# One pass over the weights for both segments in w_out and the last w_down chunk, with every second scaled norm tile in PSUM

## Chip, cores and metric

The kernel runs on one core of a Trainium2 chip. The metric is device time in microseconds (us), the median of several runs. The profile is one further execution, recorded by the hardware profiler. Engines: PE is TensorE (PEld its weight loads), DVE is VectorE, ACT is ScalarE, POOL is GpSimd, SP issues the DMAs.

## What is computed

A two-layer diffusion trunk on 512 latent tokens and 256 context tokens of 1024 features. Each layer mixes tokens (attention of three kinds and a short convolution), projects the result with w_out, adds it to x with a gate, norms x, and runs a gated FFN with a convolution over the tokens. The parts that matter here, cut from the reference:

```python
def rmsnorm(x, w):
    return x * lax.rsqrt(jnp.mean(x * x, axis=-1, keepdims=True) + EPS) * w
...
for l in range(DEPTH):
    need_ctx = l < DEPTH - 1
    hl = modulate(rmsnorm(xl, norm_mix_w[l]), sh1, sc1) @ w_in[l]
    ...
    yl = jnp.concatenate([oa_l, ob_l, oc_l, od_l], axis=-1) @ w_out[l]
    xl = xl + g1 * yl
    fl = modulate(rmsnorm(xl, norm_ffn_w[l]), sh2, sc2)
    xl = xl + g2 * conv_ffn(fl, ffn_w_up[l], ffn_conv_w[l], ffn_conv_b[l], ffn_w_down[l])
    if need_ctx:
        ...
return rmsnorm(xl, final_norm_w)
```

In the cut, `oa_l` to `od_l` are the mixing's outputs, and the branch on `need_ctx` does the same for the context tokens. The context tokens pass through layer 0 and are only read in layer 1's mixing, so layer 1's w_out and FFN run over the 512 latent tokens alone.

## The kernel before

x lies feature-major: eight tiles `x[k]` of 128 features x 768 tokens. An fp32 product is made of three faster matmuls: a weight tile is split into a high part `wh` (a cast on ACT, L481) and the rest `wl` (a subtraction, L486, on POOL, or in the "fast" form 640 columns on DVE and 384 on POOL), an activation into `yh` and `yl` likewise, and `product` adds wh·yh, wh·yl and wl·yh for each of 8 blocks k of the contraction (24 matmuls a feature and segment; 21 in the last w_down chunk, which has 7 blocks). The weights come in the order of `unit_order`, through three `raw` buffers and two of each part.

Layer 0 works on the segments 0:512 and 512:768 (SEGS), layer 1 on 0:256 and 256:512 (HALVES). In four stages the program before makes two sweeps over the eight output features, one for each segment, and loads and splits the weights in each: w_out of layer 0, the last w_down chunk of layer 0, w_out of layer 1, and the last w_down chunk of layer 1. A product lands in a PSUM bank with the tag `tp` (there are two), and `residual` (L917, DVE) adds it to x.

After the first sweep, the norm of the first segment starts. `rstd_steps` squares x on ACT (L344), adds the eight squares on POOL and DVE (L353, the form that is not `direct`), sums over partitions with four small matmuls into `ms`, takes the root (L357, ACT) and the reciprocal (L358, DVE) and broadcasts it with four matmuls into a PSUM bank `rb` with the tag `pj` (there is one). `norm_apply` then makes for each feature tile the scaled tile `yt` = x·A·rb on DVE (L404), its high part on ACT (L408) and its low part on DVE (L414, even k) or POOL (L410 and L412, odd k). These steps are a generator; `tick` runs some of them behind each product of the second sweep and pins the DVE instructions in program order. The second segment is normed in the `direct` form (each square goes to PE, 8 groups of four `ms` matmuls), and `woven` puts its steps between pieces of the next products on the first segment: the first two FFN units (`up_open`, `up_product`), or the first w_in units. In layer 1's last stage the norm is the final one (`final`, L425), whose result `ot` goes out by DMA. `u` is a pool of six SBUF buffers that squares, `yt`, `ot` and FFN tiles share. In layer 0's FFN, rows of the modulation (`junk` and `mrow`, L311) are computed on DVE between units, in the pool `mrow`; they need `cbc`, which is loaded and put through a silu on ACT (L216) before the FFN.

Of the kernel before, what the change touches and what calls it, by code (L numbers as in the profile page):

```python
# [16 lines left out]
KT = 8  # L17
# [27 lines left out]
AHEAD_SCORES = 2  # L45
SCORE_SHARE = 0.4
# [6 lines left out]
class Trunk:  # L53
# [34 lines left out]
    def build(self):  # L88
# [53 lines left out]
        for j in range(4):  # L142
# [11 lines left out]
            for sg, rb in zip(SEGS, r):  # L154
                self.norm_apply(x, y, sg, self.amix[0], self.mod[0][:, 0:8], rb, ks)
# [14 lines left out]
        for l in range(DEPTH):  # L170
# [22 lines left out]
            y = None  # L193
# [12 lines left out]
            self.pin = ALL  # L206
            for u in first:
                part(u, 0, 8)()
# [10 lines left out]
            def after(sg, l=l, need=need, x=x, y2=y2):  # L219
                if need:  # L220
                    if not y2:
                        self.scale_vec(l + 1, self.amix[l + 1], O_NM, 8)
                        y2.extend(self.new_y())
                    steps = self.norm_steps(x, y2, sg, self.amix[l + 1], self.mod[l + 1][:, 0:8], sg != segs[0])
                    if sg == segs[0]:
                        self.pace = steps
                        self.tick(1)
                    else:
                        early = self.early_start(l + 1, True)
                        part = lambda n, k0, k1: lambda: self.early_products([early[n]], y2, SEGS[0], range(k0, k1))  # L230
                        self.woven(steps, part(0, 0, 4), part(0, 4, 8), part(1, 0, 8))
                        self.early_products(early[1:], y2, SEGS[1], range(KT))
                        self.split_weights(spare=True)
                    if sg[1] <= SEQ:
                        for k in range(KT):
                            nc.sync.dma_start(out=xd[:, k, sg[0]:sg[1]], in_=x[k][:, sg[0]:sg[1]])
                else:
                    self.pace = self.final(x, sg, sg != segs[0])
                    self.tick(1 if sg == segs[0] else 99)

            self.ffn(l, x, y, segs, first, todo, after)
# [124 lines left out]
    def norm_steps(self, x, y, sg, A, sh, direct=False):  # L366
        r = yield from self.rstd_steps(x, *sg, direct)
        for k in range(KT):
            self.norm_apply(x, y, sg, A, sh, r, [k])
            yield  # L370

# [24 lines left out]
    def norm_apply(self, x, y, sg, A, sh, r, ks):  # L396
        nc = self.nc
        a, b = sg
        n = b - a
        j = 0 if b <= SEQ else 1  # L400
        for k in ks:
            t = self.u.tile([128, T], F32, tag="u", name="yt")
            yh, yl, _ = y[k]
            i = nc.vector.scalar_tensor_tensor(out=t[:, :n], in0=x[k][:, a:b], scalar=A[:, k, j:j + 1],  # L404
                                               in1=r[:, :n], op0=ALU.mult, op1=ALU.mult)
            if self.ticking:
                self.tc.keep_in_program_order(i)
            nc.scalar.activation(out=yh[:, a:b], in_=t[:, :n], func=AF.Identity, bias=sh[:, k, j:j + 1])  # L408
            if self.slow and k % 2:
                nc.gpsimd.tensor_tensor(out=t[:, :n], in0=t[:, :n],  # L410
                                        in1=sh[:, k, j:j + 1].broadcast_to([128, n]), op=ALU.add)
                nc.gpsimd.tensor_tensor(out=yl[:, a:b], in0=t[:, :n], in1=f32v(yh[:, a:b]), op=ALU.subtract)  # L412
            else:
                nc.vector.scalar_tensor_tensor(out=yl[:, a:b], in0=t[:, :n], scalar=sh[:, k, j:j + 1],  # L414
                                               in1=f32v(yh[:, a:b]), op0=ALU.add, op1=ALU.subtract)

    def final(self, x, sg, direct):
# [3 lines left out]
        r = yield from self.rstd_steps(x, a, b, direct)  # L421
# [11 lines left out]
    def unit_order(self):  # L433

        for l in range(DEPTH):
            for u in UNITS:
                yield ("win", l, u)
            segs = SEGS if l < DEPTH - 1 else HALVES
            for _ in segs:
                for m in range(KT):  # L440
                    yield ("wout", l, m)
            for k0, k1 in CHUNKS:
                for i in range(k0, k1):
                    if i == 0:
                        yield ("wup", l, 0, 0)
                    yield ("wup", l, i, 1)
                    if i + 1 < NF:
                        yield ("wup", l, i + 1, 0)
                for _ in range(len(segs) if k1 == NF else 1):
                    for m in range(KT):  # L450
                        yield ("wdn", l, m, k0, k1)
# [469 lines left out]
    def w_out(self, l, s, x, sg):  # L921
        a, b = sg
        for m in range(KT):
            w = self.weights(("wout", l, m), b - a == 256, m % 3 == 2 and l == 0)
            p = self.bank("tp", "po")
            self.product(p[:, :b - a], w, s, a, b)
            self.residual(p, x, self.mod[l][:, 16:24], m, a, b)
            self.tick(2 if m < 3 else 1)
        self.tick(KT)
# [31 lines left out]
    def ffn(self, l, x, y, segs, first, todo, after):  # L961
# [10 lines left out]
        for k0, k1 in CHUNKS:  # L972
# [18 lines left out]
            sweeps = [[sg] for sg in segs] if k1 == NF else [cseg]  # L991
            for sweep in sweeps:
                for m in range(KT):
                    w = self.weights(("wdn", l, m, k0, k1), sweep[0][1] - sweep[0][0] == 256,
                                     k1 == NF and m % 3 == 2 and l == 1)
                    for a, b in sweep:
                        p = self.bank("tp", "pd")
                        if k1 < NF and a == SEQ:
                            self.product2(p, w, G, a, b)
                            self.residual(p, x, gate, m, a, b, 2)  # L1000
                        else:
                            self.product(p[:, :b - a], w, G, a, b)
                            self.residual(p, x, gate, m, a, b)
                    if todo and m % 2:
                        todo.pop(0)()
                    self.tick(2 if m < 3 else 1)
                self.tick(KT)
                if k1 == NF:
                    after(sweep[0])
# [439 lines left out]
```

## Time and profile before

| | |
|---|---|
| time, median of 3 runs | 1758.03 us (1757.46 to 1758.92) |
| time of the profiled execution | 1758.37 us, span 1756.6 us |
| PE busy | 1672.1 us, 95% |
| DVE, ACT, POOL busy | 952.0, 801.0, 1002.0 us |
| DMA | 244.15 MB, 139 GB/s |

PE is busy nearly all the time, so time is lost where PE waits, where its list has more matmuls than needed, or where its clock is granted at half speed. The chain of work that ended last runs through PE for the most part. The windows view shows the four stages one by one; the waits view says what PE waited for in them.

### The profile page before, as it was taken

What the parts mean: (1) busy time and instruction counts of PE and PEld (TensorE: products, weight loads), DVE (VectorE), ACT (ScalarE), POOL (GpSimd) and SP (SyncE); (2) the same over time, 40 slices, a digit from 0 to 9 for tenths busy, and PEclk for the clock granted to TensorE, in tenths of its full rate; (3) what the DMA queues carried; (4) which work ended last, traced back from release to release, by engine and by line L of the source; (5) the groups of instructions that cost most, each with busy time, mean ns of one, the idle gap of its engine ahead of it and who ended that gap; (6) DMA issues with size and microseconds to landing.
All of it is one profiled execution on the core that took longest, in us unless ns stands there. A gap on an engine that the chain in (4) does not pass through costs nothing. (4 is left out here: it accounts for less than half of the span.)

```text
span 1756.6 us, 26615 instructions
## 1 busy us (share of the span) xinstructions
PE 1672.1 (95%) x9740; PEld 1421.0 (81%) x9740; DVE 952.0 (54%) x1849; ACT 801.0 (46%) x1399; POOL 1002.0 (57%) x1348
## 2 busy tenths in 40 slices
PE   6899999899999999999999988999999999999997
PEld 4578878798878888888888877888879888888887
DVE  3577767562667754654355475877656422122245
ACT  4276766553443321332143354776654543242343
POOL 1424234776566654664467664434865776676763
PEclk9999999999999999999999999999999999999999
DMA  8566535336434433443333636453446323233334
GB/s 335 177 197 210 157 108 186 94 121 233 149 104 129 123 109 98 133 127 111 110 131 116 196 120 189 138 148 105 141 128 210 109 96 94 99 94 99 96 108 132
DMA packets 78450, 244.15 MB, mean 139 GB/s; under 512 B 9072, under 2 KB 12656, under 8 KB 78192
## 3 DMA queue, kind: packets, MB, share of 16 engines
q1 hardware_dynamic: 78320, 242.46, 43.6%
q8 instruction: 77, 1.26, 0.3%
q14 instruction: 53, 0.43, 0.1%
HBM read 214.64 MB, written 27.79 MB: 138 GB/s over the span
## 5 line engine op out<-in xcount | busy, mean ns | idle before, releaser
L486 POOL TENSOR_TENSOR wl<-raw,wh 128x256 fp32r<-128x256 f32 (+1 forms) x750 | 579.9, 803 | 556.1 <-ACT wh L481 528.5
L73 PE MATMUL pu<-y,wh 128*128 128x512 f32 (+1 forms) x1792 | 559.2, 388 | 4.2 <-DVE up L957 2.6
L481 ACT CAST wh<-raw 128x1024 fp32r<-128x1024 f32 (+1 forms) x228 | 233.6, 1027 | 353.8 <-PE pd L73 188.7
L73 PEld LDWEIGHTS pu<-y,wh 128*128 128x128 f32 x1792 | 331.8, 188 | 71.2 <-ACT wh L481 2.4
L73 PE MATMUL pu<-y,wl 128*128 128x512 f32 (+1 forms) x1072 | 369.0, 351 | 0.0
L73 PE MATMUL pj<-y,wh 128*128 128x512 f32 (+1 forms) x1216 | 325.4, 356 | 8.9 <-ACT ev L581 5.3
L73 PE MATMUL pd<-g,wh 128*128 128x512 f32 (+1 forms) x1048 | 290.2, 362 | 4.4 <-DVE x L917 2.8
L73 PEld LDWEIGHTS pj<-y,wh 128*128 128x128 f32 x1216 | 206.9, 192 | 39.1 <-ACT ev L581 8.2
L73 PEld LDWEIGHTS pu<-y,wl 128*128 128x128 f32 x1072 | 201.9, 188 | 31.1
L73 PEld LDWEIGHTS pd<-g,wh 128*128 128x128 f32 x1048 | 188.5, 193 | 34.2 <-ACT wh L481 4.0
L73 PE MATMUL pj<-y,wl 128*128 128x512 f32 (+1 forms) x608 | 212.0, 349 | 0.0
L954 DVE SCALAR_TENSOR_TENSOR up<-pu,par,up 128x511 f32<-128x511 f32 (+1 forms) x132 | 83.1, 658 | 231.4 <-ACT up L952 212.9
L73 PE MATMUL pd<-g,wl 128*128 128x512 f32 (+1 forms) x584 | 196.2, 342 | 2.9 <-DVE wl L486 2.8
L917 DVE SCALAR_TENSOR_TENSOR x<-pd,mod,x 128x256 f32<-128x256 f32 (+1 forms) x96 | 56.6, 592 | 168.9 <-PE pd L73 168.3
L73 PEld LDWEIGHTS pj<-y,wl 128*128 128x128 f32 x608 | 116.7, 192 | 14.5
L677 POOL TENSOR_TENSOR p<-p,rec 128x512 f32<-128x512 f32 (+2 forms) x80 | 79.5, 998 | 83.2 <-DVE rec L673 59.5
L73 PEld LDWEIGHTS pd<-g,wl 128*128 128x128 f32 x584 | 112.6, 193 | 17.3 <-DVE wl L486 3.5
L311 DVE SCALAR_TENSOR_TENSOR junk<-mrow,cbc 128x1024 f32<-128x1024 f32 x80 | 121.9, 1524 | 2.1 <-DMA mrow<-in_wmodt 1.3
L73 PE MATMUL po<-og,wh 128*128 128x256 f32 (+1 forms) x512 | 111.6, 314 | 3.9 <-ACT sq L344 2.5
L979 POOL TENSOR_TENSOR up<-up 128x256 f32<-128x256 f32 x105 | 105.3, 1028 | 1.4 <-DVE up L957 0.7
L748 DVE TENSOR_TENSOR wtl<-wtp,wth 128x512 fp32r<-128x512 f32 x132 | 87.4, 668 | 29.5 <-ACT wth L747 28.7
L73 PEld LDWEIGHTS po<-og,wh 128*128 128x128 f32 x512 | 84.8, 193 | 10.2 <-ACT sq L344 2.7
(174 smaller groups left out, 2370.8 us busy)
## 6 DMA issues: line engine op xcount, KB each, us to landing
raw<-in_wup SPq DMA_DIRECT2D x88, 512.0 KB, 3.4
mrow<-in_wmodt SPq DMA_DIRECT2D x56, 512.0 KB, 3.7
raw<-in_win SPq DMA_DIRECT2D x44, 512.0 KB, 3.6
raw<-in_wdn SPq DMA_DIRECT2D x48, 448.0 KB, 3.3
mraw<-in_wmod SPq DMA_DIRECT2D x40, 512.0 KB, 7.2
raw<-in_wout SPq DMA_DIRECT2D x32, 512.0 KB, 3.5
qk<-hl SPq DMA_DIRECT2D x16, 768.0 KB, 3.6
stk<-qk SPq DMA_DIRECT2D x32, 384.0 KB, 5.4
```

The lines of the kernel that those rows point to most:

```text
L73: i = self.nc.tensor.matmul(out, **kw)
L311: self.tc.keep_in_program_order(nc.vector.scalar_tensor_tensor(out=junk, in0=raw, scalar=1.0, in1=self.cbc[:, i], op0=ALU.mult, op1=ALU.mu ...
L481: i = nc.scalar.copy(out=wh, in_=raw)
L486: eng.tensor_tensor(out=wl[:, a:b], in0=raw[:, a:b], in1=f32v(wh[:, a:b]), op=ALU.subtract)
L677: self.nc.gpsimd.tensor_tensor(out=p, in0=p, in1=r.broadcast_to(list(p.shape)), op=ALU.mult)
L748: nc.vector.tensor_tensor(out=wl[:, :n * 256], in0=tp[:, :n * 256], in1=f32v(wh[:, :n * 256]), op=ALU.subtract)
L917: self.nc.vector.scalar_tensor_tensor(out=x[m][:, a:b], in0=p[:, c:c + n], scalar=gate[:, m, (0 if b <= SEQ else 1):(1 if b <= SEQ else 2) ...
L954: nc.vector.scalar_tensor_tensor(out=u[:, a + 1:b], in0=p[:, a:b - 1], scalar=cw[:, 0:1], in1=u[:, a + 1:b], op0=ALU.mult, op1=ALU.add)
L979: eng.tensor_tensor(out=uv[:, a:b], in0=ug[:, a:b], in1=uv[:, a:b], op=ALU.mult)
```

## The change

`sweep` replaces both sweeps: for features 0 to 4 one weight load serves both segments (in layer 1 one 512-wide product takes the place of two 256-wide ones). For features 5, 6 and 7 (HELD = 3) the first segment is done first and the weights are held, those of feature 7 in the `mrow` pool ("spare"); then the norm of the first segment starts, and the three held products on the second segment follow with one norm step behind each. Then come the squares and sums of the second segment, the opening of the next units, the remaining steps of the first norm, and `woven`, whose pieces are now one block k of both units. Both norms use the direct form. In `norm_apply`, the scaled tile of even k lies in a PSUM bank (tag `tp`), and its low part is delayed by two features. The writing of x to HBM at the end of layer 0 goes behind the early products.

```diff
@@ run, w_out @@
-            for sg in segs:
-                self.w_out(l, s, x, sg)
-                y = y or self.new_y()
-                steps = self.norm_steps(x, y, sg, self.affn[l], self.mod[l][:, 24:32], sg != segs[0])
-                if sg == segs[0]:
-                    self.pace = steps
-                    self.tick(1)
-            first = [self.up_open(l, 0, gv, True) for gv in range(2)]
...
+            steps, first = self.sweep(lambda m: ("wout", l, m), "po", s, x, self.mod[l][:, 16:24], segs, norm,
+                                      lambda: [self.up_open(l, 0, gv, True) for gv in range(2)])
             a, b = segs[0]
-            part = lambda u, k0, k1: lambda: self.up_product(u[1], u[0], y, a, b, range(k0, k1))
-            self.woven(steps, part(first[0], 0, 4), part(first[0], 4, 8), part(first[1], 0, 8))
+            part = lambda k: lambda: [self.up_product(u[1], u[0], y, a, b, range(k, k + 1)) for u in first]
+            self.woven(steps, *[part(k) for k in range(KT)])
@@ norm_apply @@
+        if self.slow and k % 2 == 0:
+            t = self.bank("tp", "yt")
+        else:
             t = self.u.tile([128, T], F32, tag="u", name="yt")
...
+        def low():
+            i = nc.vector.scalar_tensor_tensor(out=yl[:, a:b], in0=t[:, :n], scalar=sh[:, k, j:j + 1],
+                                               in1=f32v(yh[:, a:b]), op0=ALU.add, op1=ALU.subtract)
@@ instead of w_out, and of the last chunk's loop in ffn @@
+    def sweep(self, unit, name, ops, x, gate, segs, norm, opening, todo=()):
+        whole = segs if segs[1][1] == T else SEGS[:1]
...
+        kept = []
         for m in range(KT):
+            w = self.weights(unit(m), spare=m == KT - 1)
+            if m < KT - HELD:
+                for a, b in whole:
+                    one(m, w, a, b)
+            else:
+                one(m, w, *segs[0])
+                kept.append((m, w))
+            if todo and m % 2:
+                todo.pop(0)()
+        self.pace = norm(segs[0])
+        self.tick(1)
+        for m, w in kept:
+            one(m, w, *segs[1])
+            self.tick(1)
+        steps = norm(segs[1])
+        next(steps)
+        opened = opening()
+        self.tick(KT + 2)
+        return steps, opened
```

Each engine works off its own list in order. Three places of these lists follow; `po` and `pu` are the PSUM tiles of w_out and of an FFN unit's product, `sq` a square.

PE, layer 0 behind w_out, before: the root's broadcast `rb` of the second segment stands between eight blocks of the first unit and eight of the second.

```order
L73 MATMUL pu<-y,wl 128x512
L73 MATMUL ms<-sq,ones 32x64 x4
L73 MATMUL pu<-y,wh 128x512 x2
...
L73 MATMUL pu<-y,wl 128x512
L73 MATMUL rb<-rstd,ident 128x64 x4
L73 MATMUL pu<-y,wh 128x512 x2
```

PE, the same place in the change:

```order
L74 MATMUL po<-og,wl 128x256
L74 MATMUL ms<-sq,ones 32x64 x32
L74 MATMUL pu<-y,wh 128x512 x2
L74 MATMUL pu<-y,wl 128x512
L74 MATMUL pu<-y,wh 128x512 x2
L74 MATMUL pu<-y,wl 128x512
L74 MATMUL rb<-rstd,ident 128x64 x4
L74 MATMUL pu<-y,wh 128x512 x2
```

All eight groups of the second segment's `ms` now stand in one row behind the last held product, and `rb` stands behind one block of both units.

ACT, layer 0 behind w_out, before:

```order
L481 CAST wh<-raw 128x1024
L344 ACTIVATE sq<-x 128x256
L357 ACTIVATE rstd<-ms,eps 128x64
L216 ACT_TABLE_LOAD
L216 ACTIVATE cbc<-cbc 128x2048
L408 ACTIVATE y<-yt,mod_77 128x256 x8
```

ACT, the same place in the change:

```order
L420 ACTIVATE y<-yt,mod_77 128x512
L346 ACTIVATE sq<-x 128x256 x5
L217 ACT_TABLE_LOAD
L217 ACTIVATE cbc<-cbc 128x2048
L346 ACTIVATE sq<-x 128x256 x2
L420 ACTIVATE y<-yt,mod_77 128x512
L346 ACTIVATE sq<-x 128x256
L420 ACTIVATE y<-yt,mod_77 128x512 x3
L359 ACT_TABLE_LOAD
L359 ACTIVATE rstd<-ms,eps 128x64
L420 ACTIVATE y<-yt,mod_77 128x512 x3
```

The silu of `cbc` and the first segment's `y` moved in among the second segment's squares.

DVE, layer 0 behind w_out, before: scaled tiles stand between the residuals of the second sweep.

```order
L358 RECIPROCAL rstd<-rstd 128x128
L917 SCALAR_TENSOR_TENSOR x<-po,mod_77,x 128x256
L486 TENSOR_TENSOR wl<-raw,wh 128x640
L917 SCALAR_TENSOR_TENSOR x<-po,mod_77,x 128x256
L404 SCALAR_TENSOR_TENSOR yt<-x,affn_81,rb 128x512 x5
L486 TENSOR_TENSOR wl<-raw,wh 128x640
L414 SCALAR_TENSOR_TENSOR y<-yt,mod_77,y 128x512
L917 SCALAR_TENSOR_TENSOR x<-po,mod_77,x 128x256
```

DVE, the same place in the change:

```order
L360 RECIPROCAL rstd<-rstd 128x128
L932 SCALAR_TENSOR_TENSOR x<-po,mod_77,x 128x256
L416 SCALAR_TENSOR_TENSOR yt<-x,affn_81,rb 128x512
L501 TENSOR_TENSOR wl<-raw,wh 128x640
L932 SCALAR_TENSOR_TENSOR x<-po,mod_77,x 128x256
L416 SCALAR_TENSOR_TENSOR yt<-x,affn_81,rb 128x512 x2
L428 SCALAR_TENSOR_TENSOR y<-yt,mod_77,y 128x512
L416 SCALAR_TENSOR_TENSOR yt<-x,affn_81,rb 128x512 x2
...
L416 SCALAR_TENSOR_TENSOR yt<-x,affn_81,rb 128x512
L360 RECIPROCAL rstd<-rstd 128x64
```

Seven of the eight scaled tiles now stand behind the last held product's residual, and the second segment's reciprocal behind them.

## Rows read from the trace of the kernel before

**Rows 1.** Windows of PE: stretch, length, busy us (matmuls), granted clock, DMA share, GB/s.

```profile
446.50:495.70 49.20, 45.94 (x361) 0.97 0.37 132
1009.10:1056.80 47.70, 42.55 (x330) 0.93 0.37 115
1346.70:1386.50 39.80, 36.77 (x353) 1.00 0.38 120
1698.10:1746.60 48.50, 46.31 (x393) 0.96 0.46 136
1746.60:1756.60 10.00, 1.99 (x40) 0.66 0.30 106
470.00:473.00 3.00, 3.00 (x16) 0.50 0.49 171
...
1704.00:1709.00 5.00, 4.57 (x23) 0.66 0.19 39
```

**Rows 2.** Waits of PE in R1, R2 and R3: us in total, times, longest.

```profile
PE po L73 <- ACT sq L344: 2.5, 1, 2.5
...
PE ms L73 <- ACT sq L344: 1.6, 1, 1.6
...
PE po L73 <- DVE wl L486: 1.8, 2, 1.5
```

**Rows 3.** Groups of instructions in 446 to 498, by shape: busy us, mean ns.

```profile
L481 ACT CAST wh<-raw 128x1024 fp32r<-128x1024 f32 x10 | 10.5, 1049 | 10.6 <-PE po L73 8.7 <-POOL wl L486 1.3 <-POOL y L412 0.6
L486 DVE TENSOR_TENSOR wl<-raw,wh 128x640 fp32r<-128x640 f32 x8 | 9.1, 1141 | 1.7 <-ACT wh L481 1.3 <-POOL y L412 0.4
L414 DVE SCALAR_TENSOR_TENSOR y<-yt,mod,y 128x512 fp32r<-128x512 f32 x4 | 5.7, 1427 | 0.0
L404 DVE SCALAR_TENSOR_TENSOR yt<-x,affn,rb 128x512 f32<-128x512 f32 x8 | 5.6, 739 | 0.4 <-PE rb L73 0.4
L408 ACT ACTIVATE y<-yt,mod 128x512 fp32r<-128x512 f32 x8 | 5.5, 722 | 2.3 <-DVE yt L404 2.3
L344 ACT ACTIVATE sq<-x 128x256 f32<-128x256 f32 x8 | 3.0, 408 | 3.5 <-DVE y L414 3.5
L216 ACT ACTIVATE cbc<-cbc 128x2048 f32<-128x2048 f32 x1 | 1.9, 1913 | 1.0 <-DMA cbc<-in_cbc 1.0
L357 ACT ACT_TABLE_LOAD x1 | 1.3, 1283 | 0.0
...
L358 DVE RECIPROCAL rstd<-rstd 128x128 f32<-128x128 f32 x1 | 1.0, 952 | 1.1 <-ACT rstd L357 1.1
```

**Rows 4.** Timeline of PE in R1: start us, us, instruction.

```profile
443.75 0.61 PE L73 MATMUL po<-og,wh 128*128 128x512 f32 x2
444.43 0.62 PE L73 MATMUL po<-og,wh 128*128 128x512 f32 x2
...
451.14 0.40 PE L73 MATMUL po<-og,wh 128*128 128x256 f32 x2
451.38 0.28 PE L73 MATMUL po<-og,wl 128*128 128x256 f32 x1
451.59 0.42 PE L73 MATMUL ms<-sq,ones 128*32 128x128 f32 x8
451.94 0.50 PE L73 MATMUL po<-og,wh 128*128 128x256 f32 x2
...
476.69 0.77 PE L73 MATMUL ms<-sq,ones 128*32 128x64 f32 x40
477.39 0.72 PE L73 MATMUL pu<-y,wh 128*128 128x512 f32 x2
```

**Rows 5.** Tile `cbc`: time from its DMA's issue to landing.

```profile
DMA to landing us min/median/max: 6.9/6.9/6.9
```

**Rows 6.** Timeline of DVE in R4: the last gate's difference, and the end.

```profile
1703.35 0.69 DVE L983 TENSOR_TENSOR g<-up,g 128x512 fp32r<-128x512 f32 x1 [0.68 <-ACT g L981]
...
1750.35 3.22 DVE L425 SCALAR_TENSOR_TENSOR ot<-x,fin,rb 128x256 f32<-128x256 f32 x8 [1.44 <-PE rb L73]
```

More of the change, by code (lines that the diff above doesn't have):

```diff
@@ L207, in build @@
             for u in first:
-                part(u, 0, 8)()
+                self.up_product(u[1], u[0], y, a, b)
             self.pin = None
@@ L217, in build @@
             y2 = []
[L219 to L239, printed above, removed]
@@ L241, in build, with norm @@
-            self.ffn(l, x, y, segs, first, todo, after)
+            def norm(sg, l=l, need=need, x=x, y2=y2, segs=segs):
+                tag = "pj"
+                if not need:
+                    return self.final(x, sg, True, tag)
+                if not y2:
+                    self.scale_vec(l + 1, self.amix[l + 1], O_NM, 8)
+                    y2.extend(self.new_y())
+                return self.norm_steps(x, y2, sg, self.amix[l + 1], self.mod[l + 1][:, 0:8], True, tag)
+            opening = lambda l=l, need=need: self.early_start(l + 1, True) if need else None
@@ new lines, in after @@
+            def after(steps, early, need=need, x=x, y2=y2):
+                if not need:
+                    for _ in steps:
+                        pass
+                    return
+                part = lambda k: lambda: self.early_products(early, y2, SEGS[0], [k])
+                self.woven(steps, *[part(k) for k in range(KT)])
+                self.early_products(early[1:], y2, SEGS[1], range(KT))
+                self.split_weights(spare=True)
+                for k in range(KT):
+                    nc.sync.dma_start(out=xd[:, k, :SEQ], in_=x[k][:, :SEQ])
@@ L242, in build @@
+            self.ffn(l, x, y, segs, first, todo, norm, opening, after)
             y = y2
@@ L364, in rstd_steps, with norm_steps @@
         return rb
-    def norm_steps(self, x, y, sg, A, sh, direct=False):
-        r = yield from self.rstd_steps(x, *sg, direct)
+    def norm_steps(self, x, y, sg, A, sh, direct, tag):
+        r = yield from self.rstd_steps(x, *sg, direct, tag)
+        held = []
         for k in range(KT):
-            self.norm_apply(x, y, sg, A, sh, r, [k])
+            low = self.norm_apply(x, y, sg, A, sh, r, k)
+            held.append(low)
+            if k > 1 and held[k - 2]:
+                held[k - 2]()
             yield
+        for f in held[-2:]:
+            if f:
+                f()
     def tick(self, n):
@@ L437, in unit_order @@
                 yield ("win", l, u)
[L438 to L441, printed above, removed]
+            for m in range(KT):
+                yield ("wout", l, m)
             for k0, k1 in CHUNKS:
@@ L448, in unit_order @@
                         yield ("wup", l, i + 1, 0)
-                for _ in range(len(segs) if k1 == NF else 1):
-                    for m in range(KT):
-                        yield ("wdn", l, m, k0, k1)
+                for m in range(KT):
+                    yield ("wdn", l, m, k0, k1)
     def prefetch(self, depth):
@@ L919, in residual, with one @@
                                                 in1=x[m][:, a:b], op0=ALU.mult, op1=ALU.add)
-    def w_out(self, l, s, x, sg):
-        a, b = sg
-        for m in range(KT):
[L924 to L929, printed above, removed]
+    def sweep(self, unit, name, ops, x, gate, segs, norm, opening, todo=()):
+        whole = segs if segs[1][1] == T else SEGS[:1]
+        def one(m, w, a, b):
+            p = self.bank("tp", name)
+            self.product(p[:, :b - a], w, ops, a, b)
+            self.residual(p, x, gate, m, a, b)
+        kept = []
+        for m in range(KT):
+            w = self.weights(unit(m), spare=m == KT - 1)
[17 more added lines that the diff above has]
+        return steps, opened
     def up_open(self, l, i, gv, fast=False):
@@ L959, in up, with ffn @@
         return u
-    def ffn(self, l, x, y, segs, first, todo, after):
+    def ffn(self, l, x, y, segs, first, todo, norm, opening, after):
         nc = self.nc
@@ L990, in ffn @@
                     todo.pop(0)()
[L991 to L1009, printed above, removed]
+            if k1 == NF:
+                after(*self.sweep(lambda m: ("wdn", l, m, k0, k1), "pd", G, x, gate, segs, norm, opening, todo))
+                continue
+            for m in range(KT):
+                w = self.weights(("wdn", l, m, k0, k1))
+                for a, b in cseg:
+                    p = self.bank("tp", "pd")
+                    if a == SEQ:
+                        self.product2(p, w, G, a, b)
+                        self.residual(p, x, gate, m, a, b, 2)
+                    else:
+                        self.product(p[:, :b - a], w, G, a, b)
+                        self.residual(p, x, gate, m, a, b)
+                if todo and m % 2:
+                    todo.pop(0)()
 class Group:
```

39 lines of the change are left out of this document (22 added, 17 removed).

## Prediction, made before the change was run

> **What bounds the kernel now.** I read the windows view of TensorE (PE) first, over the four places that the change touches; I call them R1 (w_out of layer 0), R2 (last w_down chunk of layer 0), R3 (w_out of layer 1) and R4 (last w_down chunk of layer 1, then the final norm). For R1 to R3 a window begins where feature 7's product on the first segment ends (T below) and ends with the last early product on the new features; for R4 it is the whole stage, and the tail behind it has a row too [rows 1]. PE is busy in 45.94 of 49.20 us, 42.55 of 47.70, 36.77 of 39.80 and 46.31 of 48.50, so in each the time is PE's work plus a few waits, and only what shortens PE's list or its waits counts. The waits view names them: 2.5 us for a square in R1, 1.6 for one in R2, 1.8 for split weights in R3 [rows 2]. The third thing is the granted clock: 0.50 (1.2 GHz instead of 2.4) right behind the 2.5 us wait and 0.66 around the start of R4 [rows 1]. A 256-wide matmul takes 0.12 us there at full clock (two in 451.14 to 451.38), a 512-wide one 0.227 (three in 443.75 to 444.43) [rows 4].
>
> So the second sweep's weight casts and subtractions, which the change removes (32 loads of half a megabyte, 32 casts of 1.05 us [rows 3], their subtractions on DVE and POOL), are mostly work beside PE. What the second sweep gave PE was length: eight products of 24 x 0.12 = 2.88 us, 23 us in all, under which the first segment's norm ran.
>
> **The change, part by part.** *Work on PE.* In R1 and R2 the products are the same matmuls. In layer 1, five features go in one 512-wide product instead of two of 256: 0.24 - 0.227 = 0.013 us a pair, times 5 x 24 and 5 x 21, gives -1.6 (R3) and -1.4 (R4). The first segment's squares are now summed on PE: seven more groups of four `ms` matmuls at each of four places. Set between products a group costs 0.44 us (the product behind it starts at 451.94, not at 451.50), in a burst 0.14 (five groups in 476.69 to 477.39) [rows 4]. By where the order puts them I add +1.3 (R1, 2.5 groups before T), +2.9 (R2), +2.2 (R3), +1.1 (R4); the bounds for all 28 are 3.9 and 12.3.
>
> *R1 behind T.* Five of the eight second-segment products now lie before T, so what is left of the 49.2 is 49.2 - 5 x 2.88 = 34.8. The new order, with each engine's queue in order and T = 0: burst of `ms` 1.15; held product 5 until 4.05, `ms` of k = 7, held 6 until 7.35. Meanwhile ACT casts an up weight (it needs product 5's buffer, 4.05 to 5.2), loads a table (1.28), takes the root, DVE the reciprocal (0.95) [rows 3]: 7.85, `rb` 8.7, a wait of 0.55. Held 7 ends at 11.6. Now PE needs the second segment's last square. In ACT's queue stand: y of k = 0 (0.72) from 9.5, five squares (0.41 each) to 12.35, table load 1.28, the silu of `cbc` (1.91), two squares, y of k = 1, the last square [rows 3]. The `cbc` load is issued some 7 us behind T, when an up weight's split frees a buffer, and takes 6.9 us to land [rows 5], so the silu ends at about 16 and the last square at 17.6: PE, done with the other `ms` at 12.5, waits about 5. Before, that silu stood behind the last square.
> Part k = 0 of both units: 6 x 0.227 = 1.36, to 19.1. Next in PE's order is the second segment's `rb`, and behind it parts 1 to 7. It needs the reciprocal, which on DVE stands behind seven of the first segment's scaled tiles (0.74 each [rows 3]) and three low parts; low 2 waits for y of k = 2, which ACT reaches after that last square, at 18.3. So DVE comes to the reciprocal at 22 and PE to `rb` at 22.6 to 23: a wait of 3.6. Then 7 x 1.36 = 9.5, to 33.4; both units' second segments, 5.6, to 39; and for waits of 5 and 3.6 us one stretch at half clock, 1.8 (before, 1.5 behind the 2.5 us wait: 3.0 us at 0.50; 4.57 busy us at 0.66 are 1.6 [rows 1]). 40.8 against 34.8: +6.0, with `ms` before T **+7.3**.
>
> *R2.* Left of before: 47.7 - 5 x 2.52 = 35.1. Held 7 ends at 10.2, the last square's `ms` at 16.25 (ACT's queue holds the cast of an input weight that waits for product 7, whose spare buffers it takes; wait about 5), part 0 to 17.6, `rb` at 21.8 (a modulation row of about 1.2 us on DVE now waits for the same spare buffers; wait 4.15), then 0.85, 9.5 and 2.8 with 1.8 of half clock: 37.3, +2.2. With `ms` +2.9. The first product now covers the last gate chain less (5.4 + 0.8 us of products before the last k, instead of 8.2), +1.0; the early products finish with more of the rope chain behind them, -1.3. **+4.8.**
>
> *R3.* Left: 39.8 - 14.4 = 25.4. Held 7 ends at 10.8, last `ms` 13.85 (wait 2.5; no silu here), part 0 (0.72) 14.6, `rb` 17.3 (wait 1.9), parts to 22.4, the two second segments 2.88 each: 28.2, +2.8. With `ms` +2.2, merging -1.6, and the first weights' waits gone, -1.0: **+2.4.**
>
> *R4.* The new list: 36 products of 512 before the gate's last k (8.2 us, more than its chain, which before ended on DVE at 1703.35 + 0.69, 5.9 us behind the stage's start [rows 6], so the start's waits and its half clock go), 1.36 for that k, three further features at 4.76 and a fourth in it, six products of 2.52: 38.9 in all, `ms` and `rb` 4.0, small waits 0.6: 43.5 against 48.5, -5.0. Behind it the second half's reciprocal now stands behind six of the first half's eight `ot` on DVE, which wait for buffers that the last `ms` free: 10.0 becomes about 11.8 (eight `ot` take 3.22 [rows 6]). **-3.2.**
>
> *PSUM temporaries.* The low part of an even k reads its temporary from PSUM. Before, with two SBUF operands, it took 1.43 us in the mean in R1 against 0.74 for a scaled tile, which reads `rb` from PSUM [rows 3]; I take 0.74 from that row, and if 1.43 stays, three lows ahead of `rb` are +2.1 a place. The Trainium skill (SBUF — State Buffer, Who interferes with whom) says that a DVE instruction with at most one SBUF input does not contend with GpSimd; the two rows fit it, and by it the smaller price holds. The two banks belong to the products and are empty behind held 7; a temporary waits for the low part of two even k before, which is in the queue above.
>
> *Free ends.* The 32 loads less (15 MB) and the spill of x moved behind the stage: nothing on the path; SP's queue gets shorter, and the later spill has all of the mixing before its reader. What it costs if that cover fails: a transfer, some 4 us.
>
> Sum: 7.3 + 4.8 + 2.4 - 3.2 = +11.3 us. On the profiled run's own 1758.4 that is 1769.7; its median is 0.3 lower, 1769.4.
>
> **The rivals.** *A, faster.* PE's six waits behind the held products (5 + 3.6, 5 + 4.15, 2.5 + 1.9 = 22.2 us, with 3.6 of half clock) are where I place the loss. They come from how ACT and DVE work off their queues; should those two engines, with 32 casts and all of DVE's 640-wide splits gone (eight took 9.1 us in R1 alone), run ahead by one product, the last squares and the reciprocal would be there in time. It decides at 11 us for all of it: below, the change is over 3.5 us faster; with 8 left it gives 1752. For it speaks that PE's own list is shorter in R4; against it, that the first segment's tiles k = 1 to 7 stand on DVE behind the last held product's residual in the order, whatever its load. *B, no change.* The waits come to half, 12 us with one half clock: 1758. *C, much slower.* Half clock follows each of the six waits, and `cbc` lands later than 14: four more stretches at 1.6 and 2 us, 1778. *D, the change doesn't do what it says:* excluded by the order (112 more `ms`, 225 fewer products, 32 fewer loads).
>
> **How the numbers follow.** The forecast with its neighbours (1763 to 1775) 0.60, A 0.13, B 0.14, C 0.13. A measurement of this kernel tells 0.2% (3.5 us) from no change. Faster by more: A, 0.13. Within: most of B, 0.12. Slower: 0.75. The unknown prices reach from 9 us less (no half clock, `ms` all at burst price, `cbc` early) to 8.5 more, so the range is 1757 to 1778; it leaves out A and half of C.
>
> **What would show it.** In the changed profile's waits: PE waiting for a square, around 5 us, in R1 and R2, and for the rstd reciprocal 2 to 4 us in R1 to R3; granted clock near 0.5 behind one of the two; R4 5 us shorter and the tail longer; low parts of even k at 0.7 to 0.8. If PE waits less than 1 us for `rb` in each place, the prediction falls to A.

## The result, and the profile after

The change makes the kernel slower: 1775.88 us (1772.38 to 1777.16, five runs) against 1758.92 us (1757.46 to 1762.12) for the kernel before on the same chip, a ratio of 1.0088 with a 95% interval of 1.0072 to 1.0103, so 12.7 to 18.1 us more. The forecast was 1769.4 us with a range of 1757 to 1778. The profiled execution took 1776.16 us, its span is 1774.3 us, 17.7 more than before.

Outside the four stages both kernels have the same instructions in the same order, but for a few neighbours that change places, so the shift of an instruction there (its start in the trace after less its start before, the median over DVE and ACT instructions of a stretch) tells what the stages ahead of it cost. It is 1.70 us ahead of R1, 11.83 behind it, 11.61 ahead of R2, 17.37 behind it, 18.77 ahead of R3, 19.11 behind it and 17.71 at the end:

| us over the kernel before | R1 | R2 | R3 | R4 and tail | outside | sum |
|---|---|---|---|---|---|---|
| forecast | +7.3 | +4.8 | +2.4 | -3.2 | 0 | +11.3 |
| profiled execution | +10.1 | +5.8 | +0.3 | -1.4 | +2.9 | +17.7 |

Of the 2.9 us outside, 1.7 lie ahead of R1 and are not the change's: in the profiled executions below, the same code ahead of R1 is shifted by -2.6 to +1.7. Another 1.4 lie in layer 1's mixing. There the other kernels that carry the change in layer 0 read 0.0 to 2.1, and the two without it (e7, e11) 0.2 and 0.5, so a part of these may be the change's. Two profiles differ inside a stage too: the order of instructions in R2 is, again but for a few neighbours, the same in the changed kernel and in e1, and R2 reads +5.8 in one and +8.4 in the other, so a difference of less than 3 us in R2 between two single profiles tells nothing.

The windows of PE, as in [rows 1], for the same stretches of the changed kernel (from T to the end of the early products in R1, R2, R3; the stage and the tail of R4), and then two stretches of the clock:

```profile
465.50:505.90 40.40, 35.04 (x277) 0.87 0.21 79
1038.60:1076.20 37.60, 31.44 (x232) 0.82 0.27 88
1376.00:1405.60 29.60, 27.05 (x273) 0.94 0.11 37
1717.20:1762.30 45.10, 44.59 (x308) 1.00 0.16 49
1762.30:1774.30 12.00, 3.59 (x73) 0.63 0.50 175
...
482.00:492.20 10.20, 8.36 (x34) 0.50 0.04 16
...
1052.00:1065.70 13.70, 9.80 (x55) 0.50 0.17 56
```

The lengths 40.4, 37.6, 29.6, 45.1 and 12.0 stand against 40.8, 37.3, 28.2, 43.5 and 11.8 worked out in the prediction. But the clock column differs from what was reckoned: one stretch of 10.2 us at 0.50 in R1 and one of 13.7 us in R2. The kernel before, with 0.97 and 0.93 in the mean, has shorter ones at these places, of 3.4 and 6.8 us:

```profile
469.80:473.20 3.40, 3.40 (x18) 0.50 0.45 154
1026.20:1033.00 6.80, 6.20 (x29) 0.50 0.34 102
```

What PE waited for, in R1 and R2 behind T (compare [rows 2]):

```profile
PE ms L74 <- ACT sq L346: 3.7, 2, 3.1
PE rb L74 <- DVE rstd L360: 1.6, 2, 1.2
```

```profile
PE rb L74 <- DVE rstd L360: 3.6, 2, 2.9
PE ms L74 <- ACT sq L346: 2.5, 3, 1.5
```

These are the waits that were foretold, each shorter than reckoned. The timeline of ACT in R1 shows why the last square is late (start us, us, instruction; the idle time ahead of it in brackets):

```profile
476.20 1.63 ACT L346 ACTIVATE sq<-x 128x256 f32<-128x256 f32 x5
477.85 1.28 ACT L217 ACT_TABLE_LOAD   x1
479.14 1.91 ACT L217 ACTIVATE cbc<-cbc 128x2048 f32<-128x2048 f32 x1
480.96 0.70 ACT L346 ACTIVATE sq<-x 128x256 f32<-128x256 f32 x2
481.57 0.70 ACT L420 ACTIVATE y<-yt,mod 128x512 fp32r<-128x512 f32 x1
482.18 0.40 ACT L346 ACTIVATE sq<-x 128x256 f32<-128x256 f32 x1
```

Five squares, then the table load and the silu of `cbc`, then the other squares: ACT did not even idle for the `cbc` load. PE in the same place:

```profile
477.57 0.77 PE L74 MATMUL ms<-sq,ones 128*32 128x64 f32 x40
481.41 0.63 PE L74 MATMUL ms<-sq,ones 128*32 128x64 f32 x16 [3.07 <-ACT sq L346]
482.63 0.44 PE L74 MATMUL ms<-sq,ones 128*32 128x64 f32 x8 [0.60 <-ACT sq L346]
483.01 1.22 PE L74 MATMUL pu<-y,wh 128*128 128x512 f32 x2
484.02 0.63 PE L74 MATMUL pu<-y,wl 128*128 128x512 f32 x1
...
487.18 1.94 PE L74 MATMUL rb<-rstd,ident 128*128 128x64 f32 x8 [1.24 <-DVE rstd L360]
```

From 483.01 on the 512-wide matmuls stand 0.43 to 0.50 us apart, twice the 0.227 of [rows 4].

### The profile page after: what moved, and what is told of

It is laid out like the page before. It is cut to its first block, busy times and chain, and to the rows that moved or that the text cites. A ratio compares the mean times of both kernels' runs of the same rounds, so it can differ in the third digit from the quotient of the medians.

```text
span 1774.3 us, 26279 instructions
## 1 busy us (share of the span) xinstructions
PE 1691.9 (95%) x9739; PEld 1418.1 (80%) x9739; DVE 882.2 (50%) x1783; ACT 772.8 (44%) x1369; POOL 951.6 (54%) x1344
## 4 chain that ended last, share of the span: by engine, by line
PE 80%; DVE 5%; ACT 5%; DMA 4%; POOL 3%; issue 3%; SPq 0%; DVEq 0%; ACTq 0%; POOLq 0%
PE pu L74 34%; PE pd L74 16%; PE pj L74 13%; PE po L74 6%; PE pv L74 3%; DMA stk<-qk 2%; PE wtp L78 2%; PE scc L74 1%; ACT p L680 1%; POOL wl L501 1%; PE scb L74 1%; DVE nm L672 1%; ACT wh L496 1%; PE macc L74 1%; PE sca L74 1%
## 5 line engine op out<-in xcount | busy, mean ns | idle before, releaser
L501 POOL TENSOR_TENSOR wl<-raw,wh 128x256 fp32r<-128x256 f32 (+1 forms) x766 | 559.9, 763 | 615.8 <-ACT wh L496 588.9
L496 ACT CAST wh<-raw 128x1024 fp32r<-128x1024 f32 (+1 forms) x196 | 202.3, 1033 | 328.1 <-PE pd L74 183.0
L74 PE MATMUL pd<-g,wh 128*128 128x512 f32 (+1 forms) x978 | 282.9, 371 | 2.0 <-DVE x L932 0.8
L74 PEld LDWEIGHTS pd<-g,wh 128*128 128x128 f32 x978 | 176.0, 188 | 35.2 <-issue 1.6
L74 PE MATMUL pd<-g,wl 128*128 128x512 f32 (+1 forms) x549 | 187.9, 349 | 0.1
L932 DVE SCALAR_TENSOR_TENSOR x<-pd,mod,x 128x512 f32<-128x512 f32 (+1 forms) x91 | 55.7, 614 | 206.8 <-PE pd L74 206.2
L74 PEld LDWEIGHTS pd<-g,wl 128*128 128x128 f32 x549 | 103.4, 188 | 16.2 <-POOL wl L501 1.0
L74 PE MATMUL po<-og,wh 128*128 128x256 f32 (+1 forms) x432 | 106.6, 338 | 0.1
L78 PE MATMUL wtp<-ident,p 128*128 128x128 f32 x512 | 84.4, 277 | 6.7 <-DVE p L1129 3.3
```

Of the source, the lines that this page charges most:

```text
L74: i = self.nc.tensor.matmul(out, **kw)
L78: i = self.nc.tensor.transpose(out, in_, self.ident)
L496: i = nc.scalar.copy(out=wh, in_=raw)
L501: eng.tensor_tensor(out=wl[:, a:b], in0=raw[:, a:b], in1=f32v(wh[:, a:b]), op=ALU.subtract)
L932: self.nc.vector.scalar_tensor_tensor(out=x[m][:, a:b], in0=p[:, c:c + n], scalar=gate[:, m, (0 if b <= SEQ else 1):(1 if b <= SEQ else 2) ...
```

## The experiments

Two theories to begin with. W: the loss is PE waiting behind the held products for ACT and DVE, and the half clock behind these waits. L: the loss is PE's longer list, the 112 added `ms` matmuls and where they stand. All edits are to the changed kernel unless said otherwise. The stage columns are shifts in one profiled execution each, read as above; the ratio is to the kernel before on the same chip. R4 has its tail in it.

| kernel | median us | ratio, 95% interval | R1 | R2 | R3 | R4 |
|---|---|---|---|---|---|---|
| the change | 1775.88 | 1.0088, 1.0072 to 1.0103 | +10.1 | +5.8 | +0.3 | -1.4 |
| e1_silu_behind | 1773.97 | 1.0083, 1.0067 to 1.0098 | +5.8 | +8.4 | +0.4 | -2.3 |
| e2_rb_later | 1773.00 | 1.0071, 1.0051 to 1.0092 | +6.8 | +9.8 | -1.0 | -1.4 |
| e3_sums_off_pe | 1760.55 | 1.0015, 0.9998 to 1.0032 | +3.8 | +3.2 | -3.0 | -5.2 |
| e4_yt_in_sbuf | 1781.43 | 1.0129, 1.0107 to 1.0151 | +12.3 | +9.4 | +3.0 | -1.5 |
| e5_silu_and_rb | 1768.28 | 1.0048, 1.0035 to 1.0062 | +3.7 | +6.9 | -1.1 | -2.1 |
| e6_all_three | 1757.68 | 0.9988, 0.9979 to 0.9997 | +0.1 | +5.7 | -4.5 | -4.3 |
| e7_layer1_only | 1752.37 | 0.9960, 0.9947 to 0.9974 | 0.0 | -0.3 | -2.9 | -5.2 |
| e8_held_two | 1773.11 | 1.0076, 1.0060 to 1.0092 | +8.7 | +5.4 | -0.4 | -1.3 |
| e9_rows_earlier | 1774.41 | 1.0091, 1.0076 to 1.0106 | +10.4 | +4.8 | +0.4 | -2.2 |
| e10_all_four | 1755.16 | 0.9977, 0.9968 to 0.9987 | +0.1 | +5.6 | -4.4 | -4.3 |
| e11_layer1_rb_later | 1751.37 | 0.9961, 0.9949 to 0.9974 | +0.2 | -0.4 | -3.7 | -5.2 |

**e1_silu_behind.**

```diff
-                nc.scalar.activation(out=self.cbc, in_=self.cbc, func=AF.Silu)
+                tc.keep_in_program_order(nc.scalar.activation(out=self.cbc, in_=self.cbc, func=AF.Silu))
```

> The changed kernel with one edit: the silu of cbc is pinned in ACT's order, so that it (with its two table loads) stands behind the first norm's and second norm's high parts again, as it did before the change. W, the theory of waits (the loss in R1 is PE waiting behind the held products for ACT and DVE, and the half clock that follows such waits): the wait of 3.1 us for a square shrinks below 0.6, the stretch of 10.2 us at half clock in 482 to 492 shrinks to 3.4 or goes; R1 gets 4 to 8 us shorter, 1768 to 1772 us in all. L, the theory of the longer list (the loss is the 112 added ms matmuls and where they stand between products): no part of the list changes, 1775 to 1777.

R1 fell from +10.1 to +5.8, as W expected; the whole kernel hardly moved (1.0083, with intervals that overlap), since R2 reads 2.6 us more in this profile without any edit there. The time lies between the two intervals, 1768 to 1772 and 1775 to 1777, and the wait for the last square, 0.82 us, is above the 0.6 that W named; the half clock in R1 shrank to one stretch of 3.4 us, as W said. The wait did not go, it moved. PE in R1:

```profile
477.63 0.77 PE L74 MATMUL ms<-sq,ones 128*32 128x64 f32 x40
478.55 0.63 PE L74 MATMUL ms<-sq,ones 128*32 128x64 f32 x16 [0.15 <-ACT sq L346]
479.99 0.32 PE L74 MATMUL ms<-sq,ones 128*32 128x64 f32 x8 [0.82 <-ACT sq L346]
485.24 1.10 PE L74 MATMUL rb<-rstd,ident 128*128 128x64 f32 x8 [3.34 <-DVE yt L416]
```

The last square comes 2.7 us earlier, and `rb` waits 3.34 us instead of 1.24, now for the scaled tiles that still read the first `rb` in the only bank of its tag.

**e2_rb_later.**

```diff
-            self.woven(steps, *[part(k) for k in range(KT)])
+            self.woven(steps, lambda: [part(k)() for k in range(4)], *[part(k) for k in range(4, KT)])
```

(the same line at both places where it stands)

> The changed kernel with one edit: the first piece that is woven behind the second segment's sums has four blocks k of both units instead of one, so the second segment's rb stands behind four blocks in R1, R2 and R3. W: the waits for the second rstd (1.2 us in R1, 2.9 in R2, 1.35 in R3) go, and the half clock behind them gets shorter, by 1.7 to 3.4 us in each of R1 and R2; but a piece of four blocks now waits for y of k = 1 to 3 where DVE and POOL come late, which gives back 1 to 2 us. In all 3 to 8 us less, 1768 to 1773. L: 1775 to 1777.

In R1 the second wait for `rb` went (0.4 us left, at the first `rb`), while the one for a square read 4.2 us; R1 +6.8, R3 1.3 us better. In R2 the wait of 2.9 us went too and 2.5 us of waiting for POOL's low parts came, as expected. The gain of 2.9 us in the median is at the lower end of what W said; the intervals of the two ratios overlap, so it is not clear of noise, and R2 reads +9.8 in this profile.

**e5_silu_and_rb** has both edits.

> The changed kernel with the edits of e1_silu_behind and e2_rb_later together. In e1 the wait for the last square fell to 0.8 us, but the second rb then waited 3.3 us, for its bank; in e2 the wait for rb fell to 0.4, but the one for a square grew to 4.2. W: with both edits both are gone in R1, and R1 costs 3 to 5 us over the kernel before instead of 10 (5.8 in e1, 6.8 in e2), all of it the added sums; in all 1766 to 1770 us. L, with waits that only move: R1 stays at 6 or above, 1771 to 1774.

R1 is at +3.7 and 1768.28 us lies in W's interval. The waits of PE in R1 from T on:

```profile
PE ms L74 <- ACT sq L346: 1.0, 2, 0.8
PE pu L74 <- POOL y L424: 0.8, 1, 0.8
PE rb L74 <- DVE rstd L360: 0.4, 1, 0.4
```

and its window, to be held against the first row above (40.40, 35.04 busy, 0.87):

```profile
464.10:498.00 33.90, 31.60 (x277) 1.00 0.26 94
```

The same 277 recorded matmuls take 33.9 us instead of 40.4: 2.3 us of idle time instead of 5.4, and no stretch at half clock in the window, so of the 6.5 us 3.1 are waits and 3.4 are the clock. That is W, shown in R1. What is left there (+3.7) is not waits.

**e3_sums_off_pe.**

```diff
-                return self.norm_steps(x, y, sg, self.affn[l], self.mod[l][:, 24:32], True, "pj")
+                return self.norm_steps(x, y, sg, self.affn[l], self.mod[l][:, 24:32], sg != segs[0], "pj")
```

(and the same for `final` and for the norm behind w_down)

> The changed kernel with the first segment's squares added up on POOL and DVE again (as before the change), 112 ms matmuls fewer on PE. L: each of the 28 groups costs PE 0.15 to 0.55 us by its place, some 9 us in all, and no more is needed to explain the loss in R1 and R2: 1766 to 1769. W: PE's list gets shorter by the same 9 us, but the adds come later than the sums did, the waits behind the held products stay as they are and the half clock too; where a group stood beside a wait nothing is saved: 3 to 6 us less, 1770 to 1773.

15.3 us less, more than either theory said. Of the four stages, R1 gets 6.3 us shorter (with less half clock too: one stretch of 6.8 us, where the change has 10.2 and 3.4), R3 3.3, R4 3.8, R2 2.6. The list itself can be read from the residuals: from the first product of a stage to the residual of the last held product it is 74.7 us in the changed kernel and 71.1 in e3 (R1), 51.6 and 48.2 (R3), 45.2 and 42.5 (R4); in R2, to feature 7's first residual, 57.4 and 53.2. That is 3.6, 3.4, 2.7 and 4.2, 13.9 us for 28 groups, or 0.50 us a group in the mean. In R2 the gain is given back at once: with the adds on POOL and DVE the first `rb` waits 3.3 us, and the last held residual comes at 67.2 us instead of 67.9. PE's rows around one place of the changed kernel show the price (a group of four matmuls is eight records in the trace, so half a group stands here):

```profile
421.65 0.28 PE L74 MATMUL po<-og,wl 128*128 128x256 f32 x1
421.86 0.41 PE L74 MATMUL ms<-sq,ones 128*32 128x128 f32 x4
422.20 0.72 PE L74 MATMUL po<-og,wh 128*128 128x512 f32 x2
422.76 0.40 PE L74 MATMUL po<-og,wl 128*128 128x512 f32 x1
```

The product behind the place starts 0.55 us behind the one ahead of it, where 0.12 is the rule, and the two of the next row take 0.56 to the third where 0.45 is the rule: 0.43 + 0.11 = 0.54 us. A place in R2 where a whole group stands costs hardly more, 0.45 + 0.11 = 0.56 us:

```profile
997.85 0.28 PE L74 MATMUL pd<-g,wl 128*128 128x256 f32 x1
998.06 0.43 PE L74 MATMUL ms<-sq,ones 128*32 128x128 f32 x8
998.42 0.72 PE L74 MATMUL pd<-g,wh 128*128 128x512 f32 x2
998.98 0.40 PE L74 MATMUL pd<-g,wl 128*128 128x512 f32 x1
```

So the price goes by the place and hardly by how many matmuls stand there. The order sets R1's groups ahead of T in four places and a burst; read in this way, all places that the change has more than e3 add up to 3.6 us in R1 and 4.2 in R2, as the residuals say. (In R3 and R4, with `ms` 64 wide, most places cost 0.42 to 0.45 us, and the sums are 3.7 and 3.7 against 3.4 and 2.7.)

**e6_all_three** has the edits of e1, e2 and e3.

> The changed kernel with the edits of e1, e2 and e3 together. e3 took 15 us off. W with L: R1 comes to 0 to 2 us over the kernel before (3.8 in e3, of which 4 us are waits and their clock), R2 stays 2 to 4 over, R3 3 and R4 5 under: 1753 to 1757 us. If the waits only move: as e3, 1759 to 1761.

R1 is at +0.1: the waits with their clock (6.5) and the sums (3.6) together are the 10.1 us of R1. R3 and R4 are 4.5 and 4.3 us under the kernel before. R2 stayed at +5.7, above what was expected, and so did the time, at 1757.68 us. The gains of e5 (7.6 us) and e3 (15.3) do not add up in e6 (18.2); what stops R2 is read under e10.

**e4_yt_in_sbuf.**

```diff
-        if self.slow and k % 2 == 0:
-            t = self.bank("tp", "yt")
-        else:
+        if True:
             t = self.u.tile([128, T], F32, tag="u", name="yt")
```

> The changed kernel with all scaled tiles in SBUF, the delay of the low parts kept. If the PSUM temporaries pay: the low parts of even k, which read two SBUF operands again, take 1.2 to 1.8 us beside POOL instead of 0.75, the second reciprocal comes 1 to 3 us later in R1 to R3, 3 to 8 us more in all, 1779 to 1784. If PSUM temporaries are what holds the norm up (two banks, each waiting for a low part): 2 to 4 us less, 1772 to 1774. W alone, if DVE is not what the second rb waits for: no change.

5.6 us slower than the change: the PSUM temporaries pay. The low parts of even k in R1, by shape, first in the changed kernel and then in e4:

```profile
L428 DVE SCALAR_TENSOR_TENSOR y<-yt,mod,y 128x512 fp32r<-128x512 f32 x4 | 3.0, 748 | 1.9 <-ACT y L420 1.9
```

```profile
L426 DVE SCALAR_TENSOR_TENSOR y<-yt,mod,y 128x512 fp32r<-128x512 f32 x4 | 4.7, 1177 | 0.5 <-ACT y L418 0.5
```

0.75 us with a PSUM operand against 1.18 with two SBUF operands (1.43 in [rows 3], with more POOL work beside it). The mean hides two prices. Two of e4's four low parts run while POOL works and take 1.77 and 1.55 us, the other two, with POOL idle for most of their time, 0.74 and 0.65; the change's four take 0.75 each, three of them beside POOL. Two rows of e4:

```profile
482.07 1.77 DVE L426 SCALAR_TENSOR_TENSOR y<-yt,mod,y 128x512 fp32r<-128x512 f32 x1 [0.49 <-ACT y L418]
487.68 0.65 DVE L426 SCALAR_TENSOR_TENSOR y<-yt,mod,y 128x512 fp32r<-128x512 f32 x1
```

(Of the four 256-wide ones of e4 only one was slowed beside POOL, 0.83 us against 0.48.) This agrees with what the Trainium skill (SBUF — State Buffer, Who interferes with whom) says of a DVE instruction with at most one SBUF input beside GpSimd. Not all of the 5.6 us need be this: with eight instead of four scaled tiles in the six buffers of `u`, DVE's scaled tiles in R1 also waited 1.8 us for ACT's high parts and 1.1 us for a square, which they did not in the change. The two were not tested apart.

**e8_held_two.** `HELD = 2`.

> The changed kernel with two features held instead of three: one product on the second segment (2.9 us in R1 and R3, 2.5 in R2) goes ahead of T and no longer covers the first segment's rstd and rb. W: that cover is what is short, PE's waits behind the held products grow by 1 to 2.9 us in each of R1 to R3, with half clock 3 to 9 us more in all, 1779 to 1785 us. L: the list is the same, 1775 to 1777.

A miss for W's second half. The time did not rise (1773.11 us; R1 +8.7). PE in R1 waited not at all for a square, 3.2 us for `rb` and 2.0 us for parts of y. With two held, feature 5's product and its square on the second segment stand ahead of T as well. The time lies below the intervals of both theories, and the interval of its ratio overlaps the change's. So the length of the cover, three products or two, is not what decides; that the order on ACT and DVE does is shown by e1, e2 and e5, not by this run.

**e9_rows_earlier.**

```diff
-            if todo and m % 2:
+            if todo and m in (0, 1, 3, 5):
```

> The changed kernel with one edit: in the sweeps of w_down the modulation rows stand behind features 0, 1, 3 and 5 instead of 1, 3, 5 and 7, so no row waits for the buffers that hold feature 7's weights, and no row stands among the scaled tiles on DVE in R2. W: DVE's wait of 1.9 us and the row's 1.2 us go, the wait for the second rb in R2 (2.9 us) falls below 1 and the half clock of 13.7 us gets shorter: R2 3 to 6 us less, 1770 to 1773 in all. L: 1775 to 1777.

The modulation row left the place among R2's scaled tiles, DVE's wait of 1.9 us for it and PE's 2.9 us wait for the second `rb` are gone (0.8 left, at the first `rb`), and the first rope step behind the early products starts 87.2 us behind the stage's start instead of 92.2. Yet R2 is only 1.0 us better (+4.8), and the ratio, 1.0091, is that of the change: a miss. The trace shows where the 5 us go. `hl`, the split queries and keys, is written to HBM and loaded back in another layout as `stk` for the scores `sca`. On the way to it DVE's rope steps now wait for the rope table's load and for POOL, whose own rope step stands behind seven small ones that wait for another load, and PE then waits 6.66 us for `stk`:

```profile
1069.64 0.69 DVE L615 TENSOR_TENSOR rot<-rot,rope 128x512 f32<-128x512 f32 x1 [1.56 <-DMA rope<-in_rope]
1070.13 1.57 POOL L1313 TENSOR_TENSOR bf<-rpb,maskc 128x32 f32<-128x32 f32 x7 [4.12 <-DMA rpb<-in_rpb]
1072.99 0.69 DVE L616 TENSOR_TENSOR ev<-ev,rot 128x512 f32<-128x512 f32 x1 [2.66 <-POOL ev L614]
1092.62 1.62 PE L74 MATMUL sca<-stk 128*128 128x512 f32 x4 [6.66 <-DMA stk<-qk]
```

The same wait in the changed kernel, and in the kernel before:

```profile
1095.05 0.95 PE L74 MATMUL sca<-stk 128*128 128x512 f32 x4 [3.02 <-DMA stk<-qk]
```

```profile
1078.84 0.94 PE L73 MATMUL sca<-stk 128*128 128x512 f32 x4 [1.54 <-DMA stk<-qk]
```

The scores start 112.5 us behind the stage's start instead of 113.8, and PE is at half clock for 10.2 us in 1088 to 1098, around the end of this wait, where the change has 3.4.

**e10_all_four** is e6 with that edit.

> e6_all_three with the edit of e9. R2 costs 5.7 us over the kernel before in e6, with 3.3 us of waiting for the first segment's rb and 2.3 for the low parts of y. W: without the row among the scaled tiles R2 falls to 2 to 4 us over, 1753 to 1756 in all. If the row is hidden behind other waits: as e6, 1757 to 1758.

1755.16 us, in W's interval and 0.9977 of the kernel before; but R2 is at +5.6 and not 2 to 4 over, and against e6's 0.9988 the gain is not clear of noise. The wait for `stk` is there again:

```profile
1082.54 1.62 PE L74 MATMUL sca<-stk 128*128 128x512 f32 x4 [6.13 <-DMA stk<-qk]
```

The scores start 112.1 us behind the stage's start, as they do in e3, e6 and e9 (112.4, 112.4, 112.5), against 109.2 in the kernel before. What the edits take off PE's waits ahead of the early products comes back, for the most part, as a longer wait for this load. Of R2's 5.6 us 2.9 are the later scores, and most of the rest is the clock: around the end of this wait PE is at 0.50 for 6.8 us, in which it is busy for 5.76. Why the load ends later than in the kernel before was not tested.

**e7_layer1_only and e11_layer1_rb_later** start from the kernel before and take the single pass in layer 1 alone, with the first squares summed on POOL and DVE; e11 has e2's edit in R3 as well. The core of the edit to `run` and `ffn` of the kernel before:

```diff
+            if not need:
+                steps, first = self.sweep(lambda m: ("wout", l, m), "po", s, x, self.mod[l][:, 16:24], segs, norm,
+                                          lambda: [self.up_open(l, 0, gv, True) for gv in range(2)])
...
+            if k1 == NF and NT < T:
+                steps, _ = self.sweep(lambda m: ("wdn", l, m, k0, k1), "pd", G, x, gate, segs,
+                                      lambda sg: self.final(x, sg, sg != segs[0]), lambda: None, todo)
```

> The kernel before, with the single pass in layer 1 only (R3 and R4, the wide products) and the first segment's squares off PE as in e3; R1 and R2 in the old order of instructions. Both theories expect the sum of two stages of e3: R3 2.5 to 3.5 us and R4 4.5 to 5.5 us under the kernel before, 1749 to 1752 us. If the gain of a stage in e3 was only the clock's stretches falling otherwise: above 1754.

> e7_layer1_only with the second rb behind four blocks in R3. In e7 PE waited 1.3 us for it; where e2's edit was added to e3 (e6) R3 went from 3.0 to 4.5 us under the kernel before. W: 1 to 1.5 us less than e7, 1750.5 to 1752. L: as e7, 1752 to 1753.

1752.37 us (0.9960) and 1751.37 us (0.9961): both beat both kernels, by about the sum of the two stages. In absolute time e7 is just above its interval, but the kernel before also read 1759.86 us beside it; the profile has R3 at -2.9 and R4 at -5.2, both as expected. e11's R3 is 0.7 us better than e7's; the times of the two can't be told apart.

## Why the prediction was right or wrong

**Right: direction and place.** PE's waits behind the held products, for the last squares behind the silu and for the second `rb` behind seven scaled tiles, are there, with the chain as worked out, and taking both away (e5) takes 6.5 us off R1. Behind T, R1 took 40.4 us (40.8 worked out) and R2 37.6 (37.3).

**Right in sum, wrong in its parts: R1 behind T.** I reckoned 9.2 us of waits (5, 3.6 and 0.55) and 1.8 us for the clock. PE waited 5.3 us (3.7 and 1.6), but was at 0.50 for 10.2 us, in which it did 8.36 us of work that would take some 4.2 at full clock (an estimate, half of it; e5's window shows 3.4 us less busy time); and the wait of 2.1 us for a convolution behind the first pair, which the kernel before has too, was followed by half clock in 509.3 to 512.7, which it was not before. "one stretch at half clock, 1.8" is the term that was too small, and it was hidden by waits that I made too long: the last square came at 482.6, 17.1 us behind T, not 17.6, and part of the time PE worked on the two groups ahead of it; the second reciprocal ended at 487.0, 21.5 us behind T instead of some 22.5, while block k = 0 took 2.9 us at half clock instead of 1.4.

**Mis-sized: the sums on PE.** "By where the order puts them I add" 1.3, 2.9, 2.2 and 1.1 us, 7.5 in all with bounds of 3.9 and 12.3; e3's list shows 13.9, outside the bounds (R1's chain behind T had a burst of 1.15 us besides, and even with it 8.7 stand against 13.9). The fault is the price of a group between products: I read 0.44 us from the start of the product behind it and left out that this product's row is longer too (in [rows 4] 0.50 us for two matmuls that take 0.40 elsewhere), and I counted groups where the price goes by the place. In R1 the 2.5 groups ahead of T stand in four places, which cost 2.2 us, as much as four groups, and not 1.3.

**R3: two errors that cancel.** It came out at +0.3 instead of +2.4. Behind T it took 29.6 us, 1.4 more than worked out. Ahead of T it was 3.0 us better than reckoned (40.4 us for 35.9 of products, where the kernel before took 29.4 for 23.0): what lay among its first products was more than the 1.0 us of weight waits that I took. Which part of it the single pass removes was not tested apart.

**R4: right in kind, too good by 1.8 us.** The waits and the half clock at the start are gone (PE is busy in all of 1715 to 1725 at a clock of 1.00), and the tail grew from 10.0 to 12.0 us as worked out: DVE does six `ot`, then the second reciprocal.

```profile
1763.02 2.44 DVE L443 SCALAR_TENSOR_TENSOR ot<-x,fin,rb 128x256 f32<-128x256 f32 x6 [0.18 <-PE ms L74]
1765.38 0.55 DVE L360 RECIPROCAL rstd<-rstd 128x64 f32<-128x64 f32 x1
1768.05 3.22 DVE L443 SCALAR_TENSOR_TENSOR ot<-x,fin,rb 128x256 f32<-128x256 f32 x8 [2.13 <-PE rb L74]
```

The stage itself took 45.1 us, not 43.5, by the sums again: 2.7 us of them, not 1.1 (e3).

**R2: right to a microsecond, by parts that partly cancel.** +5.8 against +4.8. Ahead of T it lost 5.3 us (3.9 reckoned, with 2.9 for sums that cost 4.2), behind T 2.5 (2.2 reckoned, but the terms as written add up to 36.75 and not 37.3), and behind the early products it won 2.0 back (1.3 reckoned). Behind T the waits were 5.4 us instead of 9.15 and the clock cost some 4.9 instead of 1.8, as in R1. The row on DVE that waits for the spare buffers was as foretold, and removing it (e9) removed the wait; but the time did not follow, because PE's next wait, for the load of `stk`, grew from 3.0 us to 6.7 in e9 and 6.1 in e10. The prediction has no term for this load, only "more of the rope chain behind them". What makes the load late is open.

**The rivals.** A wanted less than 11 us of waits and clock in all. The six waits came to 12.7 us (3.7 + 1.2, 2.5 + 2.9, 1.1 + 1.3) instead of 22.2, but the stretches at half clock around them cost some 4.2, 4.9 and 1.7 us in R1, R2 and R3 (half of 8.36, 9.80 and 3.40 busy us) instead of 3.6 for all: 23.5, far above A's point and near the 25.8 of the forecast. So B's waits came about (it had 12 us) together with C's clock, without C's late `cbc`, which landed 13.5 us behind T. That the sum holds is in part luck: waits that were too long stood in for a clock that was too cheap. The measured 1775.88 us is inside the range but just above the 1763 to 1775 that had the most chance, and nearer to C's 1778 than to 1769.4. (The lower end of the range, 1757, does not follow from its reason: 9 us less is 1760.) The PSUM temporaries behave as taken.

## What to carry to other kernels

A small matmul group between two products costs what it disturbs, not what it computes, here some 0.45 to 0.55 us a place for half a group as for a whole one: read its price as the time from the matmul ahead of it to the second one behind it, against the same distance without it, and keep sums in a burst or on an idle engine. When weights are loaded once for two segments, the second sweep that is saved was also the cover for the first segment's norm; then the in-order queues of ACT and DVE decide, and one foreign instruction among the squares (here the silu and its table load) or a reciprocal behind seven tiles sets when PE goes on. Before a wait is shortened, look for the one that comes next: in R2 what was won ahead went into waiting for a load. Price a wait on PE with the granted clock behind it, from rows of the same kernel, and take the gain stage by stage: here the single pass, with its sums off PE, gains 7 to 8 us in layer 1; in layer 0, even with the other edits, it gains nothing in R1 and loses some 6 us in R2.

## What the runs showed of the hardware that was not expected

In R1 PE ran at 0.50 for 10.2 us without a break from 482.0 on, right behind a wait of 3.07 us and with the waits of 0.60 and 1.24 us in it, although it was busy for 8.36 us of them; with the waits down to 1.0, 0.8 and 0.4 us (e5) the same 277 matmuls ran at 1.00 throughout. The 2.1 us wait behind the first pair of units is in every kernel; it was followed by 3.4 us at half clock in six of the thirteen profiles (the change, where it is 509.3 to 512.7, e5, e6, e8, e9 and e10) and not in the others, the kernel before among them. And stretches at half clock come and go in code that is the same: the profiled execution of the change has one at 229 us, in the attention of layer 0, that the kernel before lacks, and is 1.7 us behind from there on.
